# A four-layer hybrid trunk on one core: scheduler priorities in two mixers and an early table load

## The chip, the cores and the metric

The kernel runs on one core of one Trainium2 chip. The metric is the device time of one execution in microseconds (us): the median of repeated executions of the same program. One execution was also taken by the hardware profiler, and all rows further down come from that one. The engines of a core run side by side, each through its own list of instructions in a fixed order: PE (TensorE) does matrix products and transposes, ACT (ScalarE) activations and copies with a function table, DVE (VectorE) element work, POOL (GpSimd) element work as well, and SP (SyncE) here only issues DMAs.

## The reference

A residual stream of 256 positions by 1024 features goes through four layers. Each layer is a token mixer with an RMS norm ahead of it, and a SwiGLU block behind it:

```python
h = x
for i in range(4):
    xn = rms_norm(h, mix_norm[i])
    h = h + mixer[i](xn)       # 0: short conv, 1: recurrent, 2: attention, 3: short conv
    h = h + swiglu_ffn(rms_norm(h, ffn_norm[i]), ...)
```

The change touches layers 1 and 2 (and a buffer of the last block). The recurrent mixer has 10 blocks of 128 channels:

```python
rec = conv4(x W_rec)
r = sigmoid(rec Wa + ba); i = sigmoid(rec Wx + bx)      # per block of 128
a = exp(8 r log_sigmoid(lam)); b = sqrt(1 - a*a) * (i * rec)
s = scan(a, b)                                          # s[t] = a[t] s[t-1] + b[t]
y = (gelu(x W_gate) * s) @ w_out
```

Attention has 8 heads; queries, keys and values come from low-rank projections, and queries and keys are normalised per head, the plain part (128 wide) and the rotary part (64 wide) each for itself:

```python
q = rms_norm(c_q) @ w_uq;  kv = rms_norm(c_kv) @ w_ukv
q_nope, q_rope = rms_norm(q[:128]), rope(rms_norm(q[128:]))
k_nope, v = rms_norm(kv[:128]), kv[128:];  k_rope = rope(rms_norm(k_rope))
p = softmax(mask(q_nope k_nope' + q_rope k_rope') * scale);  y = (p v) @ w_o
```

## The kernel before

All products are made of pairs. `split` (L189, L190, or L192, L193 with a scale) casts a float32 tile to a rounded high part on ACT and takes the rest, the low part, on DVE; a product is then three matrix products, high by high, high by low, low by high (L170 to L172; L177 and L178 where high and low lie side by side). Weights are treated alike: `load_w` has SP issue the DMA into `wraw`, ACT cast it to `whi` (L84) and DVE subtract (`wlo`, L85). `prefetch` keeps eight such tiles of 128x1024 in flight, in the order of one plan for the whole program; the weights of the recurrent gates are loaded apart from it, by `gate_w`, in two DMAs for a pair of blocks.

The program is written as steps, and the Tile scheduler sets the order on each engine. It goes by priority, which is the order in which the code was written unless `tc.high_priority()` lifts what stands under it, and by its own view of what is ready. `tc.issue_after(x)` puts an instruction behind `x` on its engine. ACT holds one set of function tables at a time; `ACT_TABLE_LOAD` rows show where it changes.

**The recurrent mixer** works through `LRU_STEPS`, on pairs of blocks: `R` the recurrent projection and its convolution, `g` the gates (`gates`, two sigmoids a block, with `gate_w` of the next pair issued at their head), `c` the chain of exponential, tanh and square root with two products on DVE, `s` the scan (L625), `G` the gate branch's projection, `e` the end (`gated`): gelu on ACT (L534), the product with the scan on DVE, and `split` to `yh` (L189) and `yl` (L190). The helper `act` groups ACT's work by function: a group begins behind the last instruction of the group before (all these rows have line L534). `project_out` then multiplies `yh` and `yl` by `lru_w_out`.

**Attention** works through `MLA_STEPS`: `v` (`kv`) makes two heads of keys and values for 128 positions t: matrix products (L181 to L183), a copy of the keys to `ks` (L836), the split of the values (`xp`, L192 and L193) and two squares with their sums (L841). `n` (`q_nope`) makes two heads of queries, with `split` to `qth`, `qtl` and their squares `sqn` (L872). `u` sums the squares on PE by products with a column of ones (L739, tile `mi`). `m` (`q_norm`) makes from them the factors `fqq`: a variance on DVE, a square root on ACT (`root`, L750), reciprocal and one Newton step on DVE, the scales `fs` and `nfs` for the softmax (L889, L890), and the product with the rotary queries `q` (L894). `K` and `k` do the like for keys (roots `fk`). `d` (`k_rope_out`), `a` (`q_rope_out`) and `x` (`k_out`) transpose rotary keys, rotary queries and keys on PE into tiles of the two-bank PSUM pool `pmis` (names `mi`), from which `split` takes them to `krth`, `qrth` and `kth` and their low parts. The scores then follow (L170 to L172 on `qth`, `kth`, `qrth`, `krth`), the masked maximum on DVE, the exponential on ACT (L970), and the transposes of the probabilities `sm` (L981).

Of the kernel before, what the change touches and what calls it, by code (L numbers as in the profile page):

```python
# [9 lines left out]
F32 = mybir.dt.float32  # L10
F32R = mybir.dt.float32r
I32 = mybir.dt.int32
AF = mybir.ActivationFunctionType
ALU = mybir.AluOpType
AX = mybir.AxisListType

P = 128
# [16 lines left out]
             "r00 p08 r10 n00 p07 n02 e00 p08 p05 c00 v00 p06 u00 n06 p04 n04 v01 u04 m00 v02 v03 m04 K00 v10 a00 v11 k10 v12 a04 v13 d00 x00 x10 k14 x04 x14".split()]  # L34
# [5 lines left out]
H = 8  # L40
# [14 lines left out]
def tile_trunk(ctx: ExitStack, tc: tile.TileContext, ins: dict, out: bass.AP):  # L55
# [347 lines left out]
    def project_last(ktiles, rhs, xr):  # L403

        n = len(range(0, ktiles, KC))
        for mp in range(KD // 2):
# [4 lines left out]
            for i, ts in [(i, (t,)) for t in range(2) for i in range(n)] if end else [(i, (0, 1)) for i in range(n)]:  # L411
# [7 lines left out]
                if i == n - 1:  # L419
                    cs = slice(mp * 2 * P, (mp + 1) * 2 * P)  # L420
                    for t in ts:
                        ot = work.tile([P, 2 * P], F32, name="ot")
                        nc.vector.tensor_tensor(ot, tiles[t][:, :2 * P], xr[:, t, cs], op=ALU.add)
                        nc.sync.dma_start(out=out[0, t * P:(t + 1) * P, cs], in_=ot)
# [93 lines left out]
    def recurrent(li, c2, offs, hc):  # L518
        o_lcw, o_lcb, o_gab, o_gxb, _ = offs
        with tc.tile_pool(name=f"lr{li}", bufs=2) as pool:  # L520
# [61 lines left out]
            def gates(np_):  # L582

                if np_ + 1 < NB // 2:
                    gate_w(np_ + 1)
# [47 lines left out]
            def gated(np_):  # L633
                b2 = slice(2 * np_, 2 * np_ + 2)
                act("g", gg[:, b2, :], gg[:, b2, :], AF.Gelu_apprx_tanh)
                nc.vector.tensor_tensor(gg[:, b2, :], gg[:, b2, :], xb[:, b2, :], op=ALU.mult)
                split((yh[:, b2, :], yl[:, b2, :]), gg[:, b2, :])
# [70 lines left out]
    def mla(li, tabs):  # L708
        scale = 1.0 / math.sqrt(DN + DR)
        QK, KV = QR // P, KVR // P  # L710
        with tc.tile_pool(name=f"ml{li}", bufs=1) as pers:
# [18 lines left out]
            with tc.tile_pool(name=f"ma{li}", bufs=2) as pool:  # L730
# [15 lines left out]

                def root(y, v, shape, tag):

                    a = pool.tile(shape, F32, name=f"ra_{tag}", bufs=1)
                    nc.scalar.activation(y, v, AF.Sqrt)  # L750
# [60 lines left out]
                k2 = pool.tile([P, 2, 2, DR], F32, name="k2", bufs=1)  # L811
                nc.gpsimd.memset(k2, 0.0)

                def k_rope_out():
                    for t in range(2):
                        for e in range(2):
                            nc.gpsimd.tensor_copy(k2[:, e, e, :], k1[:, t])
                        ps = pm_tile()
                        for e in range(2):
                            nc.tensor.transpose(ps[:, e * P:(e + 1) * P], k2[:, e].rearrange("p a r -> p (a r)"), ident)  # L820
# [105 lines left out]
                def kv_w(t, n):  # L926
# [3 lines left out]

                eq = None
# [6 lines left out]
                    "K": lambda t, h0: k_norm(t, 0, H, (nc.vector, nc.vector)), "x": k_out,  # L938
                }
                for s, t, n in MLA_STEPS:  # L940
                    stages[s](t, n)
# [76 lines left out]
    def ffn(li):  # L1018
        with tc.tile_pool(name=f"ff{li}", bufs=2) as pool:
# [37 lines left out]
            if li == DEPTH - 1:  # L1057
                project_last(KF, lambda k: (hp[:, 0, k, :], hp[:, 1, k, :]), xr)
# [41 lines left out]
```

## Time and profile before

| | |
|---|---|
| median of 3 runs | 1158.46 us (1158.23 to 1158.52) |
| the profiled execution | 1157.95 us |
| its span in the trace | 1156.2 us |
| PE busy | 1135.8 us, 98% |
| DVE busy | 879.6 us, 76% |
| ACT busy | 648.4 us, 56% |
| HBM read | 202.04 MB, 176 GB/s over the span |

The span runs from the first to the last instruction of the trace; the profiled execution's own time has 1.75 us around it. Times in rows count from the span's start. In the timeline a row is a run of like instructions: start, time from the first one's start to the last one's end, engine, line, operation, tile out<-in, count, and in brackets the idle time ahead of it and what ended it. The recurrent mixer runs from about 289 to 393 us of the span and attention from about 582 to 688 us.

### The profile page before, as it was taken

The page shows a single profiled execution, that of the slowest core. Times are in us where ns is not written, and L with a number is a line of the kernel's source. Part 1 is how long each engine was busy: PE and PEld are TensorE (multiplying, and loading weights), DVE is VectorE, ACT ScalarE, POOL GpSimd, SP SyncE. Part 2 cuts the span into 40 slices and gives each one's busy share as a digit, 9 for nine tenths or more (in the row PEclk, how much of TensorE's full clock was granted, in tenths as well). Part 3 has the DMA queues.
Part 4 walks back from the last instruction along what each step waited for, and adds up shares of the span by engine and source line. Part 5 has one row for each costly group of instructions (what it writes and reads, how often), then busy time and mean ns, then how long its engine had stood idle before and what let it go on. Part 6 is the DMA issues. An engine that isn't in the chain of part 4 may idle for free.

```text
span 1156.2 us, 19325 instructions
## 1 busy us (share of the span) xinstructions
PE 1135.8 (98%) x7427; PEld 1033.5 (89%) x7427; DVE 879.6 (76%) x1398; ACT 648.4 (56%) x1010; POOL 109.6 (9%) x127
## 2 busy tenths in 40 slices
PE   9999999999998999999999899999999999999998
PEld 8998888888998988888897798888889998888998
DVE  7879988756898787876658778887667778877741
ACT  6545555544597655554458655555444445565530
POOL 0001111001000201100104010101010001010100
PEclk9999999999999999999999999999999999999999
DMA  8866566556544766656652246565566656656550
GB/s 280 271 182 189 178 182 197 169 183 201 177 130 127 216 200 188 192 165 191 173 174 92 92 142 187 183 200 179 178 193 195 186 183 183 187 179 187 163 178 19
DMA packets 211469, 204.34 MB, mean 177 GB/s; under 512 B 12778, under 2 KB 210097, under 8 KB 211377
## 3 DMA queue, kind: packets, MB, share of 16 engines
q1 hardware_dynamic: 211202, 203.05, 57.6%
q8 instruction: 58, 0.95, 0.3%
q14 instruction: 35, 0.28, 0.1%
q10 hardware_dynamic: 174, 0.06, 0.0%
HBM read 202.04 MB, written 1.05 MB: 176 GB/s over the span
## 4 chain that ended last, share of the span: by engine, by line
PE 89%; DVE 6%; ACT 3%; issue 1%; DMA 1%; SPq 0%; ACTq 0%; DVEq 0%
PE mm L177 39%; PE mm L178 20%; PE mm L170 9%; PE mm L171 9%; PE mm L172 9%; DVE wlo L85 2%; ACT whi L84 1%; PE mi L739 1%; DMA posi<-in_positions 0%; PE mi L216 0%; ACT sm L970 0%; DVE gu L1050 0%; ACT rr L534 0%; PE mm L181 0%; DMA wraw<-in_lru_gate_x_w 0%
## 5 line engine op out<-in xcount | busy, mean ns | idle before, releaser
L85 DVE TENSOR_TENSOR wlo<-wraw,whi 128x1024 fp32r<-128x1024 f32 (+3 forms) x403 | 503.8, 1254 | 182.6 <-ACT whi L84 153.1
L84 ACT ACTIVATE whi<-wraw 128x1024 fp32r<-128x1024 f32 (+3 forms) x403 | 408.3, 1018 | 268.2 <-PE mm L177 128.4
L177 PE MATMUL mm<-xp,whi 128*128 128x512 f32 x1408 | 496.5, 397 | 0.4 <-DVE xp L193 0.3
L178 PE MATMUL mm<-xp,wlo 128*128 128x256 f32 x1408 | 394.9, 280 | 0.0
L177 PEld LDWEIGHTS mm<-xp,whi 128*128 128x128 f32 x1408 | 264.1, 188 | 63.5 <-DVE xp L193 1.1
L178 PEld LDWEIGHTS mm<-xp,wlo 128*128 128x128 f32 x1408 | 266.0, 189 | 0.1
L177 PE MATMUL mm<-hp,whi 128*128 128x512 f32 x528 | 185.0, 393 | 0.0
L170 PE MATMUL mm<-xp,whi 128*128 128x256 f32 x592 | 168.0, 284 | 0.6 <-ACT whi L84 0.6
L172 PE MATMUL mm<-xp,wlo 128*128 128x256 f32 x592 | 167.8, 283 | 0.6 <-DVE wlo L85 0.5
L171 PE MATMUL mm<-xp,whi 128*128 128x256 f32 x592 | 167.7, 283 | 0.0
L178 PE MATMUL mm<-hp,wlo 128*128 128x256 f32 x528 | 147.3, 279 | 0.0
L1049 ACT COPY gu<-mm 128x256 f32<-128x256 f32 x176 | 64.3, 367 | 108.6 <-PE mm L178 108.5
L177 PEld LDWEIGHTS mm<-hp,whi 128*128 128x128 f32 x528 | 98.9, 187 | 23.7
L172 PEld LDWEIGHTS mm<-xp,wlo 128*128 128x128 f32 x592 | 113.5, 192 | 1.2 <-DVE wlo L85 1.2
L170 PEld LDWEIGHTS mm<-xp,whi 128*128 128x128 f32 x592 | 113.5, 192 | 0.9 <-ACT whi L84 0.7
L171 PEld LDWEIGHTS mm<-xp,whi 128*128 128x128 f32 x592 | 113.5, 192 | 0.1
L1054 POOL TENSOR_TENSOR s<-s,gu 128x512 f32<-128x512 f32 x44 | 59.6, 1355 | 454.7 <-DVE gu L1051 399.3
L178 PEld LDWEIGHTS mm<-hp,wlo 128*128 128x128 f32 x528 | 98.9, 187 | 0.0
L1050 DVE TENSOR_TENSOR gu<-mm,gu 128x256 f32<-128x256 f32 x176 | 73.6, 419 | 26.5 <-ACT gu L1049 26.4
L1051 DVE TENSOR_TENSOR gu<-gu,rstd 128x512 f32<-128x512 f32 x88 | 60.9, 694 | 2.6
L189 ACT ACTIVATE hp<-s 128x512 fp32r<-128x512 f32 x44 | 27.9, 633 | 51.0 <-POOL s L1054 51.0
L171 PE MATMUL mm<-wlo,hp 128*128 128x256 f32 x176 | 49.2, 280 | 0.0
(302 smaller groups left out, 1314.6 us busy)
## 6 DMA issues: line engine op xcount, KB each, us to landing
wraw<-in_ffn_w_gu SPq DMA_DIRECT2D x176, 512.0 KB, 3.6
wraw<-in_ffn_w_down SPq DMA_DIRECT2D x80, 512.0 KB, 3.5
wraw<-in_conv_w_in SPq DMA_DIRECT2D x48, 512.0 KB, 5.0
wraw<-in_lru_w_in SPq DMA_DIRECT2D x20, 512.0 KB, 4.8
wraw<-in_conv_w_out SPq DMA_DIRECT2D x16, 512.0 KB, 3.4
wraw<-in_ffn_w_down SPq DMA_DIRECT2D x16, 256.0 KB
wraw<-in_lru_w_out SPq DMA_DIRECT2D x8, 512.0 KB, 4.5
wraw<-in_mla_w_o SPq DMA_DIRECT2D x8, 512.0 KB, 3.4
```

The source lines that it names most:

```text
L84: a = nc.scalar.activation(hi[:, c], raw[:, c], AF.Copy)
L85: b = (eng or nc.vector).tensor_tensor(lo[:, c], raw[:, c], hi[:, c].bitcast(F32), op=ALU.subtract)
L170: nc.tensor.matmul(ps, ah, bh, start=start, stop=False, skip_group_check=True)
L171: nc.tensor.matmul(ps, ah, bl, start=False, stop=False, skip_group_check=True)
L172: nc.tensor.matmul(ps, al, bh, start=False, stop=stop, skip_group_check=True)
L177: nc.tensor.matmul(ps, a[0], b, start=start, stop=False, skip_group_check=True)
L178: nc.tensor.matmul(ps[:, 1], a[1], b[:, 0], start=False, stop=stop, skip_group_check=True)
L189: nc.scalar.activation(hi, src, AF.Copy)
L1049: nc.scalar.copy(gu[:, i, j], ps[:, 1])
L1050: nc.vector.tensor_tensor(gu[:, i, j], ps[:, 0], gu[:, i, j], op=ALU.add)
L1051: nc.vector.tensor_tensor(gu[:, i], gu[:, i], rb, op=ALU.mult)
L1054: nc.gpsimd.tensor_tensor(s, s, gu[:, 1], op=ALU.mult)
```

## The change

In `recurrent`, what `gated` issues and the gate weights that `gates` has loaded for the next pair stand under `tc.high_priority()`. In `mla`, the steps `v d k K x y a` stand under it; `r e n p c u m` don't. The order of the steps is another: `d00` comes earlier, and a step `y00` is new. It calls `exp_table`, an exponential of one column of ones into the new tile `etab`, behind the last instruction of the list `roots`, in which `root` now collects each square root of attention. `k2`, the tile of rotary keys that are transposed, has a copy for each t, and its four copies on POOL stand ahead of the four transposes. `project_last`, at the very end, takes its tile `ot` from the pool of its caller; both pools give it two buffers.

```diff
 MLA_STEPS = [(x[0], *(int(c) for c in x[1:])) for x in
-             "r00 p08 r10 n00 p07 n02 e00 p08 p05 c00 v00 p06 u00 n06 p04 n04 v01 u04 m00 v02 v03 m04 K00 v10 a00 v11 k10 v12 a04 v13 d00 x00 x10 k14 x04 x14".split()]
+             "r00 p08 r10 n00 p07 n02 e00 p08 p05 c00 v00 p06 u00 n06 p04 n04 v01 u04 m00 v02 v03 m04 K00 v10 a00 v11 d00 k10 v12 a04 v13 x00 x10 k14 y00 x04 x14".split()]
...
-    def project_last(ktiles, rhs, xr):
+    def project_last(ktiles, rhs, xr, pool):
...
-                        ot = work.tile([P, 2 * P], F32, name="ot")
+                        ot = pool.tile([P, 2 * P], F32, name="ot")
...
                 if np_ + 1 < NB // 2:
-                    gate_w(np_ + 1)
+                    with tc.high_priority():
+                        gate_w(np_ + 1)
...
                 b2 = slice(2 * np_, 2 * np_ + 2)
-                act("g", gg[:, b2, :], gg[:, b2, :], AF.Gelu_apprx_tanh)
-                nc.vector.tensor_tensor(gg[:, b2, :], gg[:, b2, :], xb[:, b2, :], op=ALU.mult)
-                split((yh[:, b2, :], yl[:, b2, :]), gg[:, b2, :])
+                with tc.high_priority():
+                    act("g", gg[:, b2, :], gg[:, b2, :], AF.Gelu_apprx_tanh)
+                    nc.vector.tensor_tensor(gg[:, b2, :], gg[:, b2, :], xb[:, b2, :], op=ALU.mult)
+                    split((yh[:, b2, :], yl[:, b2, :]), gg[:, b2, :])
...
+                roots = []
+
                 def root(y, v, shape, tag):
 
                     a = pool.tile(shape, F32, name=f"ra_{tag}", bufs=1)
-                    nc.scalar.activation(y, v, AF.Sqrt)
+                    roots.append(nc.scalar.activation(y, v, AF.Sqrt).ins)
...
-                k2 = pool.tile([P, 2, 2, DR], F32, name="k2", bufs=1)
+                k2 = pool.tile([P, 2, 2, 2, DR], F32, name="k2", bufs=1)
...
                     for t in range(2):
                         for e in range(2):
-                            nc.gpsimd.tensor_copy(k2[:, e, e, :], k1[:, t])
+                            nc.gpsimd.tensor_copy(k2[:, t, e, e, :], k1[:, t])
+                    for t in range(2):
                         ps = pm_tile()
                         for e in range(2):
-                            nc.tensor.transpose(ps[:, e * P:(e + 1) * P], k2[:, e].rearrange("p a r -> p (a r)"), ident)
+                            nc.tensor.transpose(ps[:, e * P:(e + 1) * P], k2[:, t, e].rearrange("p a r -> p (a r)"), ident)
...
+                def exp_table(t, n):
+
+                    with tc.issue_after(roots[-1]):
+                        nc.scalar.activation(etab, ones[:, 0:1], AF.Exp)
+
+                etab = pool.tile([P, 1], F32, name="etab", bufs=1)
...
-                    "K": lambda t, h0: k_norm(t, 0, H, (nc.vector, nc.vector)), "x": k_out,
+                    "K": lambda t, h0: k_norm(t, 0, H, (nc.vector, nc.vector)), "x": k_out, "y": exp_table,
                 }
                 for s, t, n in MLA_STEPS:
-                    stages[s](t, n)
+
+                    with tc.high_priority() if s in "vdkKxya" else nullcontext():
+                        stages[s](t, n)
```

Three places show what moves. In the rows, a line is a line of either program, so that the same instruction can stand under a line some numbers higher after the change; a number behind an underscore tells buffers of one name apart (in `fk`, the first is the root of eight heads of t = 0, the other two those of four heads each of t = 1).

ACT at the end of the recurrent mixer, before, from the square roots `rr` of the last two pairs on; `gg` are the gelus:

```order
L534 ACT_TABLE_LOAD
L534 ACTIVATE rr<-rr 128x512 x2
L84 ACTIVATE whi<-wraw 128x1024 x4
L534 ACT_TABLE_LOAD
L534 ACTIVATE gg<-gg 128x512 x3
L84 ACTIVATE whi<-wraw 128x1024
L534 ACTIVATE gg<-gg 128x512
L189 ACTIVATE yh<-gg 128x512 x2
```

The same place after the change:

```order
L534 ACT_TABLE_LOAD
L534 ACTIVATE rr<-rr 128x512 x2
L534 ACT_TABLE_LOAD
L534 ACTIVATE gg<-gg 128x512 x4
L189 ACTIVATE yh<-gg 128x512 x3
L84 ACTIVATE whi<-wraw 128x1024
L189 ACTIVATE yh<-gg 128x512
L84 ACTIVATE whi<-wraw 128x1024 x6
```

The four weight casts between roots and gelus, and the one between the gelus, now stand behind three of the four casts `yh` or further back.

ACT in attention, before, where the root of the first four query heads (`fqq`, L750) is taken:

```order
L836 ACTIVATE ks_6239<-mm 128x256
L192 ACTIVATE xp<-mm,rkv 128x256
L841 ACTIVATE sq,vk_6240<-ks_6239 128x128 x2
L750 ACTIVATE fqq<-vqq 128x16
L836 ACTIVATE ks_6241<-mm 128x256
L192 ACTIVATE xp<-mm,rkv 128x256
L750 ACTIVATE fk_6803<-vk_6240 128x8
L841 ACTIVATE sq,vk_6242<-ks_6241 128x128 x2
L189 ACTIVATE qrth<-mi 128x512
L836 ACTIVATE ks_6241<-mm 128x256
```

ACT in attention after the change, at the root of those query heads (`fqq`, now L754); L846 is the squares, L877 the squares of the last query pair:

```order
L846 ACTIVATE sq,vk_6242<-ks_6241 128x128 x6
L754 ACTIVATE fk_6861<-vk_6242 128x4
L846 ACTIVATE sq,vk_6242<-ks_6241 128x128
L192 ACTIVATE qth<-mm,c_236 128x512
L754 ACTIVATE fk_6917<-vk_6242 128x4
L939 ACT_TABLE_LOAD
L939 ACTIVATE etab<-ones 128x1
L877 ACTIVATE sqn<-mm 128x512
L754 ACT_TABLE_LOAD
L754 ACTIVATE fqq<-vqq 128x16 x2
L84 ACTIVATE whi<-wraw 128x1024 x5
L189 ACTIVATE qrth<-mi 128x512
```

The roots `fqq` of both halves of the heads now stand behind all keys, all values and `etab`, and ahead of `etab` and behind it there is a table load each. In both programs one more load stands ahead of the first exponential of the scores, so that there is one load between the first root and the first exponential of the scores before and there are three after.

DVE in attention, before, from the scales `fs` (L889) to the products with the rotary queries `q` (L894):

```order
L754 SCALAR_TENSOR_TENSOR fqq<-ra_q,fqq 128x16
L889 TENSOR_SCALAR fs<-fqq 128x4
L890 TENSOR_SCALAR nfs<-fqq 128x4
L889 TENSOR_SCALAR fs<-fqq 128x4
L890 TENSOR_SCALAR nfs<-fqq 128x4
L883 TENSOR_SCALAR vqq<-mi,vq 128x4
L891 TENSOR_TENSOR fqq<-fqq,vqq 128x8
L193 SCALAR_TENSOR_TENSOR xp<-mm,rkv,xp 128x256
L892 TENSOR_TENSOR fqq<-fqq 128x8
L883 TENSOR_SCALAR vqq<-mi,vq 128x4
L894 TENSOR_TENSOR q_6232<-q_6232,fqq 128x256
L894 TENSOR_TENSOR q_6233<-q_6233,fqq 128x256
```

DVE after the change, from the first scale `nfs` (now L895) to the first of those products (now L899):

```order
L895 TENSOR_SCALAR nfs<-fqq 128x4
L894 TENSOR_SCALAR fs<-fqq 128x4
L895 TENSOR_SCALAR nfs<-fqq 128x4
L756 SCALAR_TENSOR_TENSOR ra_q<-fqq 128x16
L85 TENSOR_TENSOR wlo<-wraw,whi 128x1024
L896 TENSOR_TENSOR fqq<-fqq,vqq 128x8
L757 TENSOR_TENSOR ra_q<-ra_q,vqq 128x16
L85 TENSOR_TENSOR wlo<-wraw,whi 128x1024
L897 TENSOR_TENSOR fqq<-fqq 128x8
L758 SCALAR_TENSOR_TENSOR fqq<-ra_q,fqq 128x16
L85 TENSOR_TENSOR wlo<-wraw,whi 128x1024
L899 TENSOR_TENSOR q_6232<-q_6232,fqq 128x256
```

Three weight splits (L85) now stand between the scales and the product, where before one value split (L193) stood.

## Rows read from the trace of the kernel before

**Rows 1.** The page's first part: engine, busy time, share of span, instructions.
```profile
PE 1135.8 (98%) x7427; PEld 1033.5 (89%) x7427; DVE 879.6 (76%) x1398; ACT 648.4 (56%) x1010; POOL 109.6 (9%) x127
```
**Rows 2.** Windows: stretch, length, busy time by engine, granted clock, DMA share, GB/s.
```profile
360.00:370.00 10.00, 7.33 (x46) 7.13 (x47) 10.00 (x16) 6.27 (x10) 0.00 (x0) 0.83 0.28 91
626.00:640.00 14.00, 11.01 (x51) 8.63 (x50) 13.38 (x43) 13.07 (x38) 0.41 (x2) 0.76 0.20 59
```
**Rows 3.** PE's waits, 290 to 420: line waited for, us, times, longest.
```profile
PE mm L170 <- ACT yh L189: 3.1, 1, 3.1
PE mm L170 <- ACT whi L84: 1.7, 1, 1.7
...
PE mm L171 <- DVE yl L190: 0.6, 1, 0.6
```
**Rows 4.** Timeline of ACT, 324 to 370: start, time, instructions, idle before.
```profile
352.08 1.15 ACT L534 ACTIVATE rr<-rr 128x512 f32<-128x512 f32 x2
353.14 3.89 ACT L84 ACTIVATE whi<-wraw 128x1024 fp32r<-128x1024 f32 x4
...
358.34 1.67 ACT L534 ACTIVATE gg<-gg 128x512 f32<-128x512 f32 x3
```
**Rows 5.** Timeline of DVE, 324 to 370.
```profile
352.75 1.30 DVE L617 SCALAR_TENSOR_TENSOR rr<-aa,rr 128x512 f32<-128x512 f32 x2 [1.89 <-ACT rr L534]
...
361.50 1.27 DVE L625 TENSOR_TENSOR_SCAN xb<-aa,xb 128x256 f32<-128x256 f32 x2
362.69 1.27 DVE L190 TENSOR_TENSOR yl<-gg,yh 128x512 fp32r<-128x512 f32 x2
```
**Rows 6.** The chain of waits, at the recurrent mixer's start: start, time, what.
```profile
295.59 3.81 DMA wraw<-in_lru_gate_x_w
```
**Rows 7.** Timeline of PE, 609 to 658.
```profile
620.67 0.40 PE L181 MATMUL mm<-whi,cth 128*128 128x512 f32 x1
621.86 1.95 PE L739 MATMUL mi<-ones,sqn 128*128 128x1 f32 x16
632.44 0.41 PE L820 MATMUL mi<-ident,k 128*128 128x128 f32 x2 [1.61 <-DVE ra_k L752]
638.01 0.58 PE L171 MATMUL mm<-ktl,qth 128*128 128x256 f32 x1 [0.31 <-DVE ktl L193]
646.21 0.28 PE L170 MATMUL mm<-krth,qrth 128*128 128x256 f32 x1
647.89 0.28 PE L172 MATMUL mm<-krth,qrtl 128*128 128x256 f32 x1
649.53 0.84 PE L981 MATMUL mi<-ident,sm 128*128 128x128 f32 x6 [1.35 <-DVE sm L974]
```
**Rows 8.** Timeline of ACT, 605 to 672.
```profile
621.19 0.61 ACT L872 ACTIVATE sqn<-mm 128x512 f32<-128x512 f32 x1
624.18 0.38 ACT L836 ACTIVATE ks<-mm 128x256 f32<-128x256 f32 x1 [1.16 <-PE mm L183]
624.46 0.47 ACT L192 ACTIVATE xp<-mm,rkv 128x256 fp32r<-128x256 f32 x1
624.82 0.31 ACT L841 ACTIVATE sq<-ks 128x128 f32<-128x128 f32 x1
625.11 0.31 ACT L841 ACTIVATE sq<-ks 128x128 f32<-128x128 f32 x1
645.05 1.28 ACT L970 ACT_TABLE_LOAD   x1 [1.51 <-DVE nm L967]
```
**Rows 9.** Timeline of DVE, 605 to 672.
```profile
621.42 0.19 DVE L752 SCALAR_TENSOR_TENSOR ra_q<-fqq 128x16 f32<-128x16 f32 x1
622.37 0.30 DVE L890 TENSOR_SCALAR nfs<-fqq 128x4 f32<-128x4 f32 x1
624.71 0.76 DVE L894 TENSOR_TENSOR q<-q,fqq 128x256 f32<-128x256 f32 x2
639.01 1.22 DVE L85 TENSOR_TENSOR wlo<-wraw,whi 128x1024 fp32r<-128x1024 f32 x1
```

More of the change, by code (lines that the diff above doesn't have):

```diff
@@ L1057, in ffn @@
             if li == DEPTH - 1:
-                project_last(KF, lambda k: (hp[:, 0, k, :], hp[:, 1, k, :]), xr)
+                project_last(KF, lambda k: (hp[:, 0, k, :], hp[:, 1, k, :]), xr, pool)
             else:
```

## Prediction

> **What bounds the kernel now.** I read the page first: TensorE (PE) is busy 98% of the span [rows 1]. So almost all of the time is matrix work that the change does not touch, and only the stretches where PE stands still or runs at a low clock can move. The waits of PE and the windows then say where: the end of the recurrent block, where PE waits 3.1 us for ACT's `yh`, 1.7 us for a gate weight's cast and 0.6 us for `yl` [rows 3], and the stretch of attention from 626 to 640 us, where PE is busy 11.01 of 14 us [rows 2]. Both also run at 1.2 GHz for a while: a granted clock of 0.83 over 10 us is 3.4 us at half speed, and 0.76 over 14 us is 6.7 us [rows 2]. The timelines of ACT and DVE around these places show which work stands ahead of what PE wants. Before the recurrent block and after attention the two programs issue the same instructions in the same order, so nothing is counted there.
>
> All sums stand on the clock of the profiled execution: 1157.95 us, with a span of 1156.2 us. The median of the three timed runs, 1158.46 us, lies 0.5 us above it; I add changes to 1157.95.
>
> **The gated tiles.** Before, ACT casts four weight tiles from 353.14 to 357.03 us between the last roots and the first gelu [rows 4], and DVE splits the same four before it multiplies the gates (the second engine's part of those 3.89 us). The change sends the four gelus, their products and their casts ahead. What is late next is DVE: after the roots it has four 512-column operations from 352.75 [rows 5], at 0.6 us each to 355.15, and then, in the new order, scan, two products, scan, two products, six operations at 0.6 us (the pace of the scans and of `yl` [rows 5]), so that the first `yl` runs from 358.75 to 359.35. Before, it ended at 363.3 (362.69 and half of its pair [rows 5]), and PE went on right behind. The gain by this chain is 4.0 us. The weights that were passed over are cast after `yh`; the first product with them waits no longer, since its own tile was cast earlier.
>
> Against it stand the gate weights. Each `gate_w` is two DMAs, a cast and a split, and all four now go ahead, on SP past one or two loads of `lru_w_out` too, which land that much later and are not needed before 359. On ACT the cast now stands ahead of a whole sigmoid group, and ACT waits in order. At the block's start the same load cost ACT 3.81 us from issue to landing [rows 6]. An early cast may meet its data at once (0) or wait for a landing whole (3.8); I take the middle, 1.9, because the load is issued earlier too. Two whole landings would turn the block's gain into a loss of 3.6; the trace has only the one place that waits, so that stays at the very edge.
>
> The low clock after the 3.1 us wait lasted 3.4 us [rows 2] and cost PE half of it, 1.7 us. With two holes of about 2 us left it may come again; I take half, 0.9. Block: 4.0 - 1.9 + 0.9 = **3.0 us gained**, between 0.2 and 5.7.
>
> **Attention's values and keys, and the exponential's table.** The new order of ACT decides here. The high-priority values and keys go first; the roots of the query norms (step `m`, not in the list of letters) are left behind, and the table load hangs on the last *key* root. So the order reads: sums, key roots, load, `etab`, the squares `sqn` of the last query pair, load, two query roots, five weight casts; and a third load where the exponentials begin. Before there was one switch from root to exponential. The load is not ahead of the path: it is on it, twice.
>
> *First stall.* PE ran out of work at 630.83 (632.44 less its wait of 1.61 [rows 7]). Of what it had done by then, eight query transposes (0.11 each, 0.9 us) and eight sums (16 in 1.8 us [rows 7], so 0.9) now come later: it is done at 629.0 and wants `sqn`. Its last pieces are 6 sums (0.7), 17 matmuls of 256 columns (0.12 each: 14 steps in 1.68 us [rows 7]) and 12 of 512 columns (0.23 each: five in 1.19 us [rows 7]), in all 5.5 us; so the five interleaved value tiles end together at 623.5, the first of them at 622.6. From there ACT has 7 copies `ks` at 0.28, 7 casts `xp` at 0.36, 14 squares at 0.29 (steps of [rows 8]), three small roots, one `qth` at 0.6, the load at 1.28 [rows 8], `etab` 0.2 and `sqn` at 0.6 [rows 8]: 11.6 us, and 0.7 of wait for the last two tiles. `sqn` ends at 634.9: PE idles 5.9 us.
>
> *Second stall.* Eight sums end at 635.8, the second load at 636.2, the second root, behind its variance, at 636.5. DVE then needs two reciprocals (0.35), seven small operations (621.42 to 622.67 [rows 9], 1.25), five more (0.8), three weight splits that the order puts in between (1.14 each [rows 9], 3.4) and half of the query product (0.4 of 0.76 [rows 9]): 6.2 us. The first query transpose starts at 642.7; PE idles 6.9 us.
>
> *From there to the scores.* The transposes of queries, rotary keys and keys share two PSUM banks, and each bank is freed by ACT and DVE. DVE has 7.2 us in order until the third key tile (among it two more splits), and PE and ACT two exposed turns of about 0.95 us (four transposes and the cast): the scores run from 651.8, where before they ran from 638.01 [rows 7]. Then 56 matmuls at 0.12 take 6.7 us and the probabilities' transposes start at 658.5, where before they started at 649.53 [rows 7]: **9.0 us lost**. The third load (1.28) lies beside those 56 matmuls and costs nothing; were they shorter by 1.1 us it would show. If the splits of the second stall cost nothing, 3.4 less: 5.6. The clock was low for 6.7 us of the old stretch and would be low for the new, longer one; what runs on into the scores costs between 0 and 56 × 0.093 = 5.2 us (0.213 in place of 0.12). I take 0.9, as in the other block: **9.9 us lost**, between 5.6 and 14.2.
>
> By the Trainium skill (ScalarE: Activation LUTs, What ACT_TABLE_LOAD costs) a switch of set is a load of some 1.28 us and a drain of 1.38 us; by it, an estimate, the two added switches would cost 5.3 in place of 2.6 us and the sum would be 2.7 us higher. The trace bears out the first figure and not the second: between cast and gelu there are 1.31 us, load included [rows 4]. The same page (Rules for kernel authors) asks that one set be finished before another is loaded, which speaks against this order of root, exponential, root, exponential.
>
> **Edits at nothing.** The zeroed `k2` doubles on POOL and its four copies go ahead of the second rotary product: POOL's work ends well before PE's transposes at 642.7, and if it did not, each copy would add its few tenths there. `ot` moves to another pool with the same two buffers. Query transposes and sums only change place.
>
> **The rivals.** *The clock stays low through the scores* (for: the stalls are longer than the old ones; against: the old low stretch ended soon after work was steady): 1157.95 + 9.0 + 5.2 - 2.1 = 1170.1. *The recurrent block pays for attention*, the way to not slower: its whole price is 1.7 + 3.1 + 0.6 of waits [rows 3] and 1.7 of low clock, 7.1 us, if the gate casts meet their data and DVE's splits leave no hole; with 9.0 lost that gives 1159.9, and it is faster only if attention costs under 7.1. For it: ACT and DVE really drop 3.9 us there; against: the chain of scans alone leaves 1.6 us. *The change does what its words say*, the query roots being done before the load: 3.0 us of idle of [rows 2] and 1.28 of load go too, 1157.95 - 3.0 - 4.3 = 1150.7; the order speaks against it. *Each load drains its engine*: two more by 1.38, 1167.6; only the skill's page named above speaks for it.
>
> **How the numbers follow.** 1157.95 + 9.9 - 3.0 = 1164.9, so 1165. Chances: forecast 0.65, low clock 0.15, block pays 0.10, words true 0.05, drain 0.05. Bounds: 1157.95 + 5.6 - 5.7 = 1157.9 and 1157.95 + 14.2 - 0.2 = 1172; the likeliest case itself lies in 1161 to 1168. For 8 in 10 I take 1159 to 1170.5, which takes in the paying block and the low clock. A difference of 0.2%, 2.3 us, is about what a measurement of this kernel can tell: slower 0.83 (the forecast but for 0.02, low clock, drain), within 0.2% 0.09 (the paying block's larger part, 0.02 of the forecast), faster 0.08.
>
> **What would show it.** Three loads after the first root in ACT's rows of attention; PE waiting about 6 us for `sqn` and about 7 for the query product; scores and `sm` some 14 and 9 us later against the block's end; in the recurrent block four gelus in a row and the PE wait for `yh` gone, with one of about 2 us for `yl`. I am wrong if PE's first stall is under 4 us (ACT then cleared the value tiles faster than its steps allow), or if the block gains nothing because ACT stands waiting for gate weights.

## The result and the profile after

The changed kernel takes 1168.94 us (median, 1167.0 to 1170.26) against 1158.49 us before: ratio 1.0088, interval 1.0072 to 1.0104, so 8.3 to 12.0 us slower. The forecast was 1165.0, in a range of 1159 to 1170.5. The profiled execution took 1167.0 us with a span of 1165.2 us.

Where the time went is read best stage by stage. The table takes each stage from its trace, from the start of the last product of the feed-forward block ahead to the start of the last product of the mixer (recurrent), and from the last product of the next feed-forward block to the first product of the one behind attention (attention).

| us | before | after | difference |
|---|---|---|---|
| ahead of the recurrent mixer | 289.1 | 290.1 | +0.9 |
| recurrent mixer | 104.1 | 100.8 | -3.2 |
| feed-forward block of layer 1 | 188.3 | 186.3 | -2.1 |
| attention | 106.1 | 119.6 | +13.6 |
| all behind it | 468.6 | 468.4 | -0.2 |

Only the mixers have another order. Together they make 10.4 us, and the medians differ by 10.45. The feed-forward block between them runs the same instructions; its 2.1 us are looked at in the last section.

The page's first part and two windows (columns as in [rows 1, 2]) of the changed kernel, the end of the recurrent mixer and the stretch of attention from the first stall to the scores:

```profile
PE 1136.8 (98%) x7427; PEld 1035.7 (89%) x7427; DVE 882.8 (76%) x1398; ACT 651.3 (56%) x1013; POOL 108.7 (9%) x127
```

```profile
355.00:365.00 10.00, 7.85 (x51) 7.45 (x51) 10.00 (x16) 9.52 (x14) 0.00 (x0) 0.83 0.03 4
624.00:652.00 28.00, 12.45 (x52) 10.19 (x52) 19.47 (x59) 16.42 (x40) 0.37 (x3) 0.57 0.30 94
```

PE is busy for 98% of the span as before and says nothing. The second window says it all: 12.45 of 28 us busy, at a granted clock of 0.57, where the 14 us of [rows 2] had 11.01 and 0.76. In the trace the clock is at half from 627.85 to 651.75 us, 23.9 us; before, it was so for 6.8 us.

PE's waits in the changed kernel, first from 290 to 420 us, then from 580 to 710 us (columns as in [rows 3]):

```profile
PE mm L171 <- DVE yl L190: 1.8, 1, 1.8
...
PE mm L170 <- ACT yh L189: 0.4, 1, 0.4
```

```profile
PE mi L906 <- DVE q L899: 6.3, 2, 6.1
PE mi L741 <- ACT sqn L877: 5.6, 1, 5.6
PE mi L825 <- DVE qrtl L190: 2.0, 1, 2.0
PE mi L863 <- DVE ktl L193: 1.4, 1, 1.4
```

The wait of [rows 3] for the gate weight's cast is gone and that for `yh` has fallen from 3.1 to 0.4 us; the one for `yl` has grown from 0.6 to 1.8 us. Attention has the two forecast stalls, on `sqn` and on the query product, and two more behind them.

The timelines of ACT, PE and DVE in attention after the change, to be held against [rows 7 to 9]:

```profile
627.45 0.21 ACT L754 ACTIVATE fk<-vk 128x4 f32<-128x4 f32 x1
627.68 1.28 ACT L939 ACT_TABLE_LOAD   x1
628.97 0.20 ACT L939 ACTIVATE etab<-ones 128x1 f32<-128x1 f32 x1
629.08 0.58 ACT L877 ACTIVATE sqn<-mm 128x512 f32<-128x512 f32 x1
629.68 1.28 ACT L754 ACT_TABLE_LOAD   x1
630.97 0.21 ACT L754 ACTIVATE fqq<-vqq 128x16 f32<-128x16 f32 x1
633.71 0.21 ACT L754 ACTIVATE fqq<-vqq 128x16 f32<-128x16 f32 x1 [2.53 <-DVE vqq L888]
...
654.29 1.28 ACT L983 ACT_TABLE_LOAD   x1 [2.14 <-DVE nm L980]
```

```profile
623.78 0.28 PE L172 MATMUL mm<-cth,wlo 128*128 128x256 f32 x1
629.71 3.58 PE L741 MATMUL mi<-ones,sqn 128*128 128x1 f32 x16 [5.65 <-ACT sqn L877]
639.36 1.15 PE L906 MATMUL mi<-ident,q 128*128 128x128 f32 x4 [6.07 <-DVE q L899]
...
642.93 0.66 PE L825 MATMUL mi<-ident,k 128*128 128x128 f32 x2 [1.99 <-DVE qrtl L190]
...
651.07 0.56 PE L171 MATMUL mm<-ktl,qth 128*128 128x256 f32 x1
...
658.91 0.85 PE L994 MATMUL mi<-ident,sm 128*128 128x128 f32 x6 [0.34 <-DVE sm L987]
```

```profile
635.07 1.22 DVE L85 TENSOR_TENSOR wlo<-wraw,whi 128x1024 fp32r<-128x1024 f32 x1
...
637.66 1.22 DVE L85 TENSOR_TENSOR wlo<-wraw,whi 128x1024 fp32r<-128x1024 f32 x1
638.80 0.75 DVE L899 TENSOR_TENSOR q<-q,fqq 128x256 f32<-128x256 f32 x2
```

The last key root, the load, `etab` and `sqn` follow each other on ACT without a gap, and PE's 16 sums start the moment `sqn` is there. The second root then waits for the sums, not for the second load. Behind it DVE's splits stand ahead of the query product, and PE's first transpose follows that product. The third load lies at 654.29 us, beside the products of the scores.

### The profile page after: what moved, and what is told of

It is laid out like the page before. It is cut to its first block, busy times and chain, and to the rows that moved or that the text cites. A ratio compares the mean times of both kernels' runs of the same rounds, so it can differ in the third digit from the quotient of the medians.

```text
span 1165.2 us, 19327 instructions
## 1 busy us (share of the span) xinstructions
PE 1136.8 (98%) x7427; PEld 1035.7 (89%) x7427; DVE 882.8 (76%) x1398; ACT 651.3 (56%) x1013; POOL 108.7 (9%) x127
## 4 chain that ended last, share of the span: by engine, by line
PE 88%; ACT 5%; DVE 4%; issue 1%; DMA 1%; SPq 0%; ACTq 0%; POOL 0%; DVEq 0%
PE mm L177 40%; PE mm L178 20%; PE mm L170 8%; PE mm L171 8%; PE mm L172 8%; DVE wlo L85 2%; ACT whi L84 1%; ACT rr L534 1%; DMA wraw<-in_lru_gate_x_w 1%; ACT L534 1%; PE mi L741 1%; DVE xp L193 0%; ACT sm L983 0%; PE mi L216 0%; PE mi L863 0%
## 5 line engine op out<-in xcount | busy, mean ns | idle before, releaser
L85 DVE TENSOR_TENSOR wlo<-wraw,whi 128x1024 fp32r<-128x1024 f32 (+3 forms) x403 | 504.4, 1256 | 177.0 <-ACT whi L84 146.0
L172 PE MATMUL mm<-whi,hp 128*128 128x256 f32 x176 | 49.2, 280 | 0.0
```

The source lines that it names most:

```text
L85: b = (eng or nc.vector).tensor_tensor(lo[:, c], raw[:, c], hi[:, c].bitcast(F32), op=ALU.subtract)
L172: nc.tensor.matmul(ps, al, bh, start=False, stop=stop, skip_group_check=True)
```

## The experiments

All ratios are against runs of the kernel before on the same chip. The stages in the tables are those of each kernel's profiled execution; a kernel's runs spread over 1 to 8 us, so a single profile carries the mechanism and the median the size.

### Which part costs what

*The recurrent part alone* has the steps of attention as before (`k2` and `ot` stay as in the changed kernel):

```diff
-             "... v11 d00 k10 v12 a04 v13 x00 x10 k14 y00 x04 x14".split()]
+             "... v11 k10 v12 a04 v13 d00 x00 x10 k14 x04 x14".split()]
...
-                    with tc.high_priority() if s in "vdkKxya" else nullcontext():
+                    with tc.high_priority() if s in "-" else nullcontext():
```

> The recurrent part alone: gated tiles and gate weights under high priority, attention's steps in the old order without priorities and without the early exponential. My theory: the two places do not touch each other, so the recurrent block ends some 2.3 us earlier, as it did in the profile of the changed kernel (391.0 against 393.3 us from the span's start), and the whole is 1156.2 us, 0.9980 of before. Rival: the weight loads that now land later take the gain back further on, and the whole is 1158.5 us, 1.000.

Measured: 1154.0 us, ratio 0.9966 (0.9954 to 0.9979).

*Attention's part alone* takes the priorities out of the recurrent mixer:

```diff
-                    with tc.high_priority():
-                        gate_w(np_ + 1)
+                    gate_w(np_ + 1)
...
-                with tc.high_priority():
+                with nullcontext():
                     act("g", gg[:, b2, :], gg[:, b2, :], AF.Gelu_apprx_tanh)
```

> Attention's part alone: new order of steps, priorities and early exponential, the recurrent mixer as before. My theory: the loss of attention stands by itself and is larger than the whole change's by what the recurrent mixer gains: from its profile (696.8 - 391.0 against 687.6 - 393.3 us) 11.5 us, so about 1170 to 1171 us, 1.010 to 1.011. Rival: the loss comes in part from weight loads that the recurrent mixer's new order has shifted, and attention alone costs under 9 us, below 1167.5 us.

Measured: 1173.68 us, ratio 1.0130 (1.0115 to 1.0145). The two parts are worth -4.2 and +15.5 us, together +11.4, and the whole change +10.5, so they add up within their intervals. Both expectations were too small, in part because I took them from where the mixers end: the first then holds the 0.9 us by which the changed kernel's mixer began later, the second the 2.1 us by which the feed-forward block between the mixers was shorter. That leaves 1.0 and 1.9 us unexplained.

*Without the gate weights*, `gated` keeps its priority. The edit, made to e1_lru_only:

```diff
-                    with tc.high_priority():
-                        gate_w(np_ + 1)
+                    gate_w(np_ + 1)
```

> The recurrent part without its gate weights: only the gated tiles under high priority, attention as before. My theory as predicted: early gate weights cost ACT time in waiting for their loads (1.9 us taken), and without them the gain is that much larger than in e1_lru_only, about 1152 us. Rival: ACT's wait for the loads lies ahead of work that is not late, and the gate weights cost nothing or even gain the 1.7 us that PE waited for the cast before: 1154 to 1155.7 us.

Measured: 1153.51 us, ratio 0.9954 (0.9938 to 0.9969). Against e1_lru_only the median shows nothing clear; the recurrent stage does: 98.2 us here and 97.9 in e3_gated_ahead_held, while the ten profiles with both priorities have 100.3 to 102.8, mean 101.3, and the two with the old order 104.1 and 104.7. ACT's wait for the gate weights' loads differs too little to be the cause: it is 4.2 us in all before, 4.5 in the changed kernel and 4.0 here. What differs is DVE's order ahead of the first `yl`, here without the scans:

```profile
355.52 0.69 DVE L631 TENSOR_TENSOR gg<-mm,rstd 128x512 f32<-128x512 f32 x1
356.12 1.89 DVE L637 TENSOR_TENSOR gg<-gg,xb 128x512 f32<-128x512 f32 x3
357.92 1.89 DVE L190 TENSOR_TENSOR yl<-gg,yh 128x512 fp32r<-128x512 f32 x3
```

The same place in the changed kernel:

```profile
356.45 0.68 DVE L626 TENSOR_TENSOR_SCAN xb<-aa,xb 128x256 f32<-128x256 f32 x1
357.05 1.27 DVE L638 TENSOR_TENSOR gg<-gg,xb 128x512 f32<-128x512 f32 x2
358.23 0.68 DVE L626 TENSOR_TENSOR_SCAN xb<-aa,xb 128x256 f32<-128x256 f32 x1
358.83 1.26 DVE L638 TENSOR_TENSOR gg<-gg,xb 128x512 f32<-128x512 f32 x2
360.02 2.49 DVE L190 TENSOR_TENSOR yl<-gg,yh 128x512 fp32r<-128x512 f32 x4
```

There PE waits 1.8 us for `yl`; here that wait does not appear, and neither does the low clock of 3.4 us that follows it there. That the place of the scans is the cause is read from the order; no run moved them alone.

### Is it the table or the order

*Without the early exponential:*

```diff
-... x00 x10 k14 y00 x04 x14".split()]
+... x00 x10 k14 x04 x14".split()]
```

> The changed kernel without the early exponential: no etab, so one table load between the roots and the scores in place of three; priorities and order of steps stay. My theory: the query factors are late because they stand behind all keys and values, and of the two added loads only the first is on the path, 1.28 us of load and 0.1 of etab; the second lies beside PE's sums. So 1.4 us less than the changed kernel, about 1167.5 us, and PE still waits some 4 us for sqn and 6 us for the query product. Rival: the changing of tables is the loss: two loads and what they delay go, 2.8 us at the least, and with them the long low clock; 1158.5 to 1164 us.

Measured: 1166.13 us, ratio 1.0065 (1.0049 to 1.0080), an interval that overlaps the changed kernel's. Attention takes 118.5 us, 1.2 less than with all three loads, and PE still waits 5.2 us for `sqn` and 5.7 for the query product. The loads are a small part of the loss. What one of them costs this run does not isolate, since the order changed with them: a query root and a weight cast now stand ahead of `sqn`, where load and `etab` stood, and counted from the first product of the query pairs the sums start only 0.5 us earlier.

```profile
628.28 1.06 ACT L84 ACTIVATE whi<-wraw 128x1024 fp32r<-128x1024 f32 x1
629.23 0.59 ACT L877 ACTIVATE sqn<-mm 128x512 f32<-128x512 f32 x1
```

*The table really ahead*, on top of e1_lru_only:

```diff
-... v13 d00 x00 x10 k14 x04 x14".split()]
+... v13 d00 x00 x10 k14 y00 x04 x14".split()]
```

> The run e1_lru_only with the early exponential put behind the last root of all (step y00 between k14 and x04 of the old order, no priorities in attention): the order of ACT then has one load between roots and scores, ahead of the scores. My theory: before, the load at 645.05 to 646.33 us stood between the first maximum and the first exponential, and PE waited 1.35 us for the probabilities behind it, so 1.3 us less than e1_lru_only, about 1154.9 us. Rival: the 56 matrix products of the scores hide the load, and PE's wait there is for the pace of maximum, exponential and product; no change against e1_lru_only, 1156.2 us.

Measured: 1152.6 us, ratio 0.9950 (0.9938 to 0.9962), 1.4 us less than e1_lru_only by medians whose intervals overlap; attention takes 105.2 us against 106.7. ACT's one load between roots and scores now stands right behind the last root; on PE the wait for the first probabilities is 0.47 us in place of the 1.35 of [rows 7]:

```profile
631.26 1.28 ACT L939 ACT_TABLE_LOAD   x1
632.56 0.20 ACT L939 ACTIVATE etab<-ones 128x1 f32<-128x1 f32 x1
```

```profile
644.65 0.85 PE L994 MATMUL mi<-ident,sm 128*128 128x128 f32 x6 [0.47 <-DVE nm L980]
```

So the idea of loading ahead is worth about a microsecond where every root is done by then.

*No priorities in attention*, all else as in the changed kernel:

```diff
-                    with tc.high_priority() if s in "vdkKxya" else nullcontext():
+                    with tc.high_priority() if s in "-" else nullcontext():
```

> The changed kernel with its new order of steps and its early exponential, but no high priority for any step of attention. ACT's order then has the query roots back among the keys and values, and one table load, ahead of the scores. My theory: the priorities, which leave the step of the query norms behind, are what costs attention its time, so all of it comes back and the early load gains its 1.3 us: as e1_table_ahead, 1152 to 1153 us. Rival: the new order of steps costs by itself (rotary keys ahead of the keys' norms), and it stays above 1156 us.

Measured: 1155.31 us, ratio 0.9968 (0.9957 to 0.9980): 13.6 us less than the changed kernel; attention takes 107.0 us against 119.6. ACT has the query roots among the keys again and one load at 628.59 us. The rival has a part in it: with the new order of steps PE waits once for 4.65 us, and attention is 1.8 us longer than in e1_table_ahead. The profiled execution took 1152.98 us, 2.3 less than the median, so that its stages may show too little of that.

```profile
631.11 1.94 PE L863 MATMUL mi<-ident,ks 128*128 128x128 f32 x8 [4.65 <-DVE ra_k L756]
```

*The query norms lifted too*, without the early exponential; the edit, made to e1_no_early_table:

```diff
-                    with tc.high_priority() if s in "vdkKxya" else nullcontext():
+                    with tc.high_priority() if s in "vdkKxyamu" else nullcontext():
```

> The run e1_no_early_table with the steps u and m, sums and factors of the queries, among those of high priority; the step n, which makes the last query pair and its squares, still is not. My theory: what is left behind is n as much as m; the factors of the first half come early, but the last pair's squares still stand behind the keys and values on ACT, so the first wait of 5 us for sqn stays, and only the splits ahead of the query product go: 3 to 4 us less than e1_no_early_table (1166.1), about 1162.5 us, still slower than before. Rival: the missing step m alone was the fault, and the kernel is back at 1155 us or below.

Measured: 1163.75 us, ratio 1.0041 (1.0027 to 1.0055), with attention at 116.2 us against 118.5. The waits are still there:

```profile
PE mi L741 <- ACT sqn L877: 5.5, 1, 5.5
PE mi L906 <- DVE q L899: 5.4, 1, 5.4
```

The first four heads' query transposes move into the time of the sums, but the last query pair, made by step `n`, still has its squares behind the keys and values, and PE's wait for the query product is now that of the second half. Step `m` alone was not what was left behind. Of the 3 to 4 us that I expected 2.4 came by the medians, whose intervals overlap, and 2.2 in attention. No run lifted `n` as well, so that the list closed over all three steps is untested.

### What stands in the second stall

*Splits held back:* the weight casts that the steps of the heads issue go behind the exponentials.

```diff
-            a = nc.scalar.activation(hi[:, c], raw[:, c], AF.Copy)
+            with tc.issue_after(hold[0]) if hold else nullcontext():
+                a = nc.scalar.activation(hi[:, c], raw[:, c], AF.Copy)
...
-                        nc.scalar.activation(sm[:, blk[t]], sm[:, blk[t]], AF.Exp, bias=nm[:, t:t + 1],
+                        hold[:] = [nc.scalar.activation(sm[:, blk[t]], sm[:, blk[t]], AF.Exp, bias=nm[:, t:t + 1],
```

> The changed kernel, with the weight casts of the output projection and of the next block that stood between the query roots and the query transposes put behind the exponentials of the first scores, so that their splits no longer stand between the scales and the query product on DVE. My theory: in the changed kernel three splits lie there from 635.07 to 638.80 us with DVE never idle, so PE's 6.1 us of wait for the query product fall to about 2.7 and the whole to about 1165.5 us, 3.4 us less than the changed kernel. Rival: the chain then waits for something else that the splits only lay beside (the roots, the banks of the transposes), and less than 1 us comes back, 1168 us.

Measured: 1163.98 us, ratio 1.0052 (1.0038 to 1.0066), and attention at 116.2 us, 3.4 less than the changed kernel (the lines of this kernel are two higher):

```profile
PE mi L743 <- ACT sqn L879: 5.7, 1, 5.7
PE mi L908 <- DVE q L901: 2.9, 1, 2.9
PE mm L172 <- ACT pt1h L191: 1.7, 1, 1.7
```

The wait for the query product falls from 6.1 to 2.9 us, one of 1.7 us appears for `pt1h`, behind the held casts. Counted from the first product of the query pairs, the probabilities' transposes start 4.8 us earlier than in the changed kernel, and 1.4 us of that is lost behind them.

*The same in the order of before*: the edit just shown, made to e1_table_ahead.

> The run e1_table_ahead (recurrent part, early exponential behind the last root, attention otherwise as before), with the same weight casts put behind the exponentials of the first scores. My theory: before the change too, splits of weights stand between the casts and the low parts of the keys on DVE (639.01 to 643.1 us and two earlier), which PE waits for in pieces of 0.3 to 0.8 us, in all some 2.5 us; about 2 us come back and the whole is about 1150.5 us. Rival: those waits are the turns of the two banks for transposes, the splits lie beside them, and what is held back is late for the output projection: 1152.6 us or more.

Measured: 1151.97 us, ratio 0.9946 (0.9931 to 0.9960). Attention takes 104.3 us against 105.2 in e1_table_ahead; the medians can't tell the two apart. The 2 us of my theory come back as far as the probabilities' transposes (1.9), and 1.0 is lost behind them, where PE waits 1.6 us for `pt1h`.

### The clock

Products without use fill PE's stalls (48 in the first run, 24 in the second). In the second run ACT and DVE keep their order. In the first, a cast of the rotary keys changes places with one of the rotary queries on ACT, and on DVE low parts of both come earlier, ahead of a weight split:

```diff
+                def fill(t, n):
+                    ps = ps_tile()
+                    for _ in range(48):
+                        nc.tensor.matmul(ps, ct[0][:, 0, :P], ct[0][:, 3:5, :].rearrange("p a s -> p (a s)"),
+                                         start=True, stop=True, skip_group_check=True)
...
-... k14 y00 x04 x14".split()]
+... k14 y00 x04 x14 z00".split()]
```

> The changed kernel with 48 products on TensorE whose result nobody reads, 512 columns each, of lowest priority: 26 of them stand ahead of the last eight sums (first stall, where PE waits 5.7 us for sqn) and 22 between these sums and the query transposes (second stall, 6.1 us); ACT and DVE keep their order. They do no useful work and can only keep PE busy. My theory: the granted clock stays at full speed where it fell to half from 627.85 to 651.75 us in the changed kernel; the eight sums then take some 1.8 us in place of 3.6, the transposes and the first scores run at the pace of before, and attention is 3 to 4.8 us shorter: about 1165 us in place of 1168.9. Rival: the chain of ACT and DVE sets the pace there and PE's clock is hidden beside it: under 1 us, 1168 us or more.

Measured: 1165.76 us, ratio 1.0060 (1.0045 to 1.0076). PE's timeline and two windows:

```profile
623.19 6.07 PE L944 MATMUL mm<-cth 128*128 128x512 f32 x26
629.10 1.85 PE L741 MATMUL mi<-ones,sqn 128*128 128x1 f32 x16
630.82 5.25 PE L944 MATMUL mm<-cth 128*128 128x512 f32 x22
637.03 0.30 PE L906 MATMUL mi<-ident,q 128*128 128x128 f32 x1 [0.96 <-DVE q L899]
```

```profile
624.00:640.00 16.00, 13.35 (x70) 10.71 (x68) 14.10 (x49) 12.46 (x32) 0.00 (x0) 1.00 0.30 88
641.00:650.00 9.00, 6.93 (x29) 5.92 (x30) 4.23 (x9) 3.23 (x5) 0.93 (x6) 0.50 0.31 97
```

The clock stays whole through both stalls, and the sums take 1.85 us in place of 3.58. Then it falls after all, behind the waits between the transposes, and the scores start at half clock. In this profile attention is 118.5 us, 1.1 less than in the changed kernel.

> The same with 24 such products, all ahead of the last eight sums, so that only the first stall is filled (24 by 0.23 us is 5.6 us); the order of all else is that of the changed kernel on every engine. My theory: the sums then run at full clock and take 1.8 us less, but the clock falls in the second stall instead, and the transposes and first scores stay slow: about 1167 us, 1.8 us less than the changed kernel. Rival: one filled stall is enough to keep the clock up to the scores: 1165 us, as with both filled.

Measured: 1163.69 us, ratio 1.0052 (1.0032 to 1.0072), over runs from 1161.15 to 1168.96. In the profiled one, which took 1168.12 us, the sums take 1.95 us and the clock is at half from 634.1 to 654.5; attention is 118.9 us. The median is nearer to the rival's time, the profile to my theory; since most runs had a higher mean clock (0.992) than the profiled one (0.990), the profile does not show what they did.

Steps counted from the first product of the query pairs, in us:

| step | changed kernel | both filled | first filled |
|---|---|---|---|
| sums end | 37.5 | 35.9 | 35.9 |
| first query transpose | 43.6 | 41.9 | 41.9 |
| scores run through | 55.3 | 53.4 | 53.7 |
| probabilities' transposes | 63.1 | 62.0 | 62.3 |

Both fillings bring the end of the sums forward by 1.6 us, and this holds as far as the scores. From the transposes to the scores the first run gains only 0.3 us more, though its first transposes ran at whole clock and its low parts came earlier: they wait for DVE (1.5 and 1.9 us), and the clock is hidden beside that. At the scores both lose 0.8 us, since the clock is at half for the first 2.4 and 3.2 us of them, against 0.7 in the changed kernel. So the profiles price the low clock at 1.6 us on the sums, and half of that is lost again at the scores: attention is 1.1 and 0.7 us shorter. By the medians the runs are 3.2 and 5.3 us shorter, with intervals that touch that of the changed kernel; what more than the stages show lies in them stays open.

### What helped, together

The recurrent part without gate weights, the table ahead, the casts held, attention otherwise as before; the edit, made to e2_ahead_and_held:

```diff
-                    with tc.high_priority():
-                        gate_w(np_ + 1)
+                    gate_w(np_ + 1)
```

> All that helped together: gated tiles under high priority without the gate weights, the early exponential behind the last root, the weight casts behind the first exponentials, attention otherwise as before. My theory: in the profiles the gated tiles alone made the recurrent block 2 to 3 us shorter than with the gate weights (98.2 against 100.3 to 102.8 us), though the medians show only 0.5; with attention at 104.3 us the whole is about 1151 us, 0.994 of before. Rival: the 98.2 us were a lucky run of the clock, gate weights cost nothing, and it is 1152 us, the same as e2_ahead_and_held.

Measured: 1149.59 us, ratio 0.9921 (0.9905 to 0.9936), faster than both kernels; its interval overlaps that of e2_ahead_and_held. Its stages are 97.9 us in the recurrent mixer and 104.5 in attention, and its 1148.7 us of span have PE busy for 99%.

```profile
PE 1133.5 (99%) x7427; PEld 1032.4 (90%) x7427; DVE 879.9 (77%) x1398; ACT 648.7 (56%) x1011; POOL 108.8 (9%) x127
```

## Why the prediction was right, and where it was not

The direction, the place and the chain of waits were right. Attention's term was too small by 3 to 4 us, and that is the 3.9 us between 1165.0 and 1168.94; the recurrent block's term came out right with the help of luck.

**The recurrent block**, forecast -3.0: the stage is 3.1 us shorter by the means above (101.27 against 104.39), but its terms missed in opposite directions. The gated tiles alone brought 6.4 us (98.03, the mean of the two profiles without early gate weights), where the forecast had 4.9 (4.0 of DVE's chain and 0.9 of clock). The gate weights cost 3.2 us, not 1.9, and not by the mechanism named: ACT's waits for landings hardly moved, the scans stand ahead of the first low parts in the runs that have them, and the wait for `yl` and the low clock follow. In the changed kernel the two together made DVE's chain to the first `yl` 3.6 us shorter (363.3 less 289.1 is 74.2 us before, 360.6 less 290.1 is 70.6 after), and the clock was at half for 3.4 us as before, so that its 0.9 did not come. PE's 1.7 us of wait for the gate weight did go with the early loads, and the waits of 0.4 and 1.8 us for `yh` and `yl` stand in their place: in e2_gated_only the first is there and the others are not.

**Attention**, forecast +9.9: 13.1 by the profiles (the stage is 106.4 us in the mean of three profiles in the old order, 119.5 in two of the new). Steps counted from the first product of the query pairs (600.17 us before, 595.81 after), in us:

| step | forecast | measured |
|---|---|---|
| PE runs dry | 28.8 | 28.2 |
| `sqn` ready, sums start | 34.7 | 33.9 |
| sums end | 35.6 | 37.5 |
| first query transpose | 42.5 | 43.6 |
| scores run through | 51.6 | 55.3 |
| probabilities' transposes | 58.3 | 63.1 |

Before, the last stood at 49.4, so that the forecast loss was 9.0 and the measured one 13.7. The stalls were sized well (5.9 and 6.9 us forecast, 5.65 and 6.07 measured), and the three loads, the wait for `yl` of about 2 us (1.8) and the four gelus in a row are there. Three terms were not sized well. The sums took 3.58 us, not 0.9, for two reasons. I had taken the 16 records of [rows 7] for 16 sums, but the trace has two records for each (52 in attention, for 26 sums in the kernel), so that eight sums are these 16 records and 1.8 us at full clock; and the clock doubled that. From the first query transpose to the scores there were four exposed waits (1.99, 0.21, 0.28, 1.35 us, 3.8 in all), not two of 0.95, and transposes at half clock. From the scores to the probabilities' transposes it was 7.8 us, not 6.7: 58 products where I had 56, a wait of 0.34 us, and the half clock of the first 0.7 us, which can cost no more than 0.4. The clock's 0.9 us failed by its place: I let it act on the scores alone and left sums and transposes at full speed, though 23.9 us of the stretch were at half. The filled runs show what it cost at the sums, 1.6 to 1.7 us. How the 2.6 us that were missing between transposes and scores divide between waits and clock stays open; in e3_filled_both, with the first transposes at whole clock, 0.3 of them came back.

**The splits** ahead of the query product, forecast at 3.4 us if they cost nothing: 3.4 us of attention came back when they were held, 4.8 gained and 1.4 lost again.

**The table**: the first load stands between the last key root and `sqn`, without a gap, and the second is hidden by the sums, as the sum's own step had it ("behind its variance"); the phrase "on it, twice" was wrong. Taking both away shortens attention by 1.2 us, with the order of ACT changed along with them. By the Trainium skill (ScalarE: Activation LUTs, What ACT_TABLE_LOAD costs) each switch also drains the engine for 1.38 us; no such gap shows here: the root ends at 627.66 us and the load starts at 627.68, `sqn` ends at 629.66 and the next load starts at 629.68. The Trainium skill's rule to do all of one set before switching (ScalarE: Activation LUTs, Rules for kernel authors) agrees in direction with those 1.2 us in e1_no_early_table, which has one load where the changed kernel has three.

**Edits at nothing**: attention with `k2` and `ot` as after and the old order took 106.7 and 106.5 us against 106.1, within what repeats.

**The rivals.** The low clock's time was the nearest (1170.1 against 1168.94), but only the number: the clock did not stay low through the scores, it rose 0.7 us into them. The drain's 1167.6 was nearer than the forecast too, and the rows just named show no drain. The block did not pay: it gained 3.1 us, where that rival had 7.1. "The words are true" would have been e1_table_ahead: 1152.6 where the rival said 1150.7; the order of the changed kernel spoke against it, and that was the right row to trust.

## What to carry to other kernels

Priority given to most steps of a chain delays the steps left out: taking it from all of them gave 13.6 us back, giving it to two of the three steps of the query norms, `u` and `m`, gave 2.4. That the list has to be closed over what the lifted steps' consumers need, here the last query pair and its factors, is what this suggests; no run closed it. A load ahead is ahead only when the issuing order puts the last user of the old table before it, which the order of the engine shows and the code does not. A stall of several microseconds should be charged twice, once as wait and once as the half clock on what PE does next, but only where PE's own work sets the pace: at the sums it cost 1.6 us here, while at the first transposes, which wait for DVE, the whole clock of one run brought 0.3.

## What was not expected of the hardware

The same feed-forward block of layer 1 took 186.3 to 186.4 us in ten of the fourteen profiles and 188.3 to 188.4 us in four, at a whole granted clock and with PE busy all but 0.6 us of the time. Its gate and up projections, the first 125 us of it, run at one of two paces, 346.7 or 353.3 ns for a pair of products; the 61.5 us of its last product are the same in all. Before and after the change, in one window:

```profile
410.00:510.00 100.00, 100.00 (x566) 86.57 (x565) 81.06 (x103) 58.48 (x91) 11.61 (x9) 1.00 0.59 183
```

```profile
410.00:510.00 100.00, 100.00 (x578) 87.43 (x578) 83.01 (x101) 60.30 (x93) 12.94 (x10) 1.00 0.62 188
```

PE is busy for all 100 us at clock 1.00 in both, with 566 and 578 products. It went with no edit: e1_table_ahead had the slow pace and e1_lru_only, the same up to attention, the fast one. What sets it stays open; it puts 2 us on single runs, as much as several of the effects above.
